# The last projection before the MLP in another order of tiles, its operand step in two parts, and new banks and loads between the MLP's two products

## The chip, the cores and the metric

One core of a Trainium2 chip runs the whole program. The metric is device time in microseconds (us), lower is better. The kernel before takes 3272.2 us (median of 3 runs, 3271.38 to 3275.03).

## The reference, cut to what matters

A decoder of two layers over 1024 tokens of width 1024. A layer has a mixing part, a cross attention and an MLP; each ends in a projection, a norm and an addition to x:

```python
        xa = cross_attention(rms_norm(x, norm_xa_pre[l]), ..., xa_wo[l])   # ends in o @ xa_wo
        x = x + rms_norm(xa, norm_xa_post[l])
        hid = jnp.square(jax.nn.relu(rms_norm(x, norm_mlp_pre[l]) @ mlp_w1[l]))
        x = x + rms_norm(hid @ mlp_w2[l], norm_mlp_post[l])
```

The change touches the way from `o @ xa_wo` into the product with `mlp_w1`, and the step from there to the product with `mlp_w2`.

## The kernel before

**Numbers.** Every matrix product is made of three matmuls, since each operand is split into a high part (a cast on ScalarE, L197) and a low part (the rest, a subtraction on VectorE, L198). A matmul of this kind is 128x128 by 128x512.

**Order.** The kernel is written as Python generators that are run one after the other or in turns (`seq(mix, xattn, after, mlp)`), over a framework that sets semaphores, gives out buffers and orders the instructions of each engine. It goes by the order of the text, but an instruction whose inputs and buffers are expected to be ready may be placed ahead of earlier ones that are not. Buffers have a tag with a fixed number of slots (`self.nb`, L101: `h` 16, `r` 16, `wr` 2, `wh` and `wl` 5, `x` 2, `xs` 2, `g` 2), and the eight banks of PSUM have the tags `d` (2), `u` (4) and `r` (2) (L102). A new buffer waits until one of its tag is free.

**The last projection** is `out_proj` (L333) with `xa_wo`, for eight tiles of 128 tokens and two halves n of 512 columns, that is 16 products of 24 matmuls. The operands of tiles 0 to 3 are formed before; those of tiles 4 to 7 (`load`, `mt`, slots of tag `r`) on the way. Half 0 makes n=0 for tiles 0 to 3, then n=1. Half 1 makes n=1 for tiles 4 to 7 first, into the banks `u`, and then n=0 for tiles 4 to 7, into the banks `d`. The n=1 weights lie in eight slots of tag `r`. When both halves of a tile are there, it is loaded (`load_x`), normed and added (`post_norm`, L295: two squares on ScalarE into a junk bank of tag `r`, a power on GpSimd, L307 and L309 on VectorE), stored, and scaled for the MLP (`scaled`, L270, into a slot `xs`: a square, GpSimd, L277). Then it is queued in `late`.

**From the queue into the MLP.** Tiles 0 to 3 are only transposed and split (`turn`, L287). The first MLP product works on 2x2 blocks by a scheme of seven products (Strassen's, in Winograd's form), and so needs, for tiles 4 to 7, sums of blocks: B22, T1, T2, T3, T4. `mlp_turn` (L1390) forms them for one tile: eight transposes into two banks of tag `r` (L1403), sums with the operands of tile tt-4 (L1415 to L1425), and a split of each of the five. It works in the tile's own `xs` slot, and reads the first of the two banks a last time at L1421. In half 1, tile 4 goes through it before the post-norm of tile 6, tile 5 before that of tile 7; 6 and 7 go through it in `finish` (L321), which makes 10 steps of the MLP (`FIN`, L30) before each.

**The MLP's first product** (`mlp`, L1429) has 16 groups g. The first two of a group's seven products, `p1` and `p2`, need only tiles 0 to 3, so for g = 0, 1, 2 these are made first, 12 matmuls each, while tiles 6 and 7 are still missing; their banks are `u`, and the weights of g = 1, 2 are loaded into slots of tag `x` (`first_weights`, L1447). Then `group` makes the five others: banks `u` for S1, S4, S2, S3 and `r` for A22, whose result VectorE takes at L1544. During group 15, `ahead` (L1643) loads and splits the first operands of the second product: `araw` from the stored hidden values `hd`, `braw` from `mlp_w2`.

**The MLP's second product** runs over blocks b and seven products each (`prods`, by the same scheme; those of b = 0 have 24 matmuls in four banks j). `sums` (L1624) forms T2, T3, T4 of the weights, on VectorE for b = 0 and on GpSimd after. The banks are chosen at L1715. The result of b = 0 is copied to `acc` by ScalarE (L1732).

All DMAs named here go through SP's queue (L137), which issues in order.

Of the kernel before, what the change touches and what calls it, by code (L numbers as in the profile page):

```python
# [8 lines left out]
F32R = mybir.dt.float32r  # L9
BF16 = mybir.dt.bfloat16  # L10
AF = mybir.ActivationFunctionType
ALU = mybir.AluOpType
# [74 lines left out]
class Kern:  # L87
# [245 lines left out]
    def out_proj(self, w, src, gpost, gpre, xin, xout, tw, tag, dst, nxt, n_nxt, first=None, early=False, pst=("uuuu", "d", "r"), turn=None):  # L333

        ws = [[], []]

        def weights(n):
            for kp in range(4):
                u = self.wunit(w[n, kp], tags=("wh", "wl") if n == 0 else (tw, tw))
                ws[n].append(tuple(t.rearrange("p (k c) -> p k c", k=2) for t in u))  # L340

        weights(0)
        yield
        gp = gn = None
        late = []

        def products(ps, n, m, ks, start, stop):
            for k in ks:
                wh, wl = ws[n][k // 2]
                self.mm3m(ps, m[0][:, k], m[1][:, k], wh[:, k % 2], wl[:, k % 2], k == start, k == stop)  # L350
                if k != ks[-1]:
                    yield

        def load(tt, i0, i1, m):
            raw = self.slot("wr", (128, 2 * (i1 - i0), 128), name="mraw")
            for i in range(i0, i1):
                self.dma(raw[:, 2 * (i - i0):2 * (i - i0) + 2],
                         src[i][:, :, 128 * tt:128 * tt + 128].rearrange("a p t -> p a t"))
            self.split(m[0][:, 2 * i0:2 * i1], m[1][:, 2 * i0:2 * i1], raw)

        operand = lambda: tuple(self.slot(tw, (128, 8, 128), F32R, name="mt") for _ in range(2))
        for half in range(2):
            ops, y0 = [], []
            if half == 0 and early:
                for j in range(4):
                    ops.append(operand())
                    load(j, 1, 4, ops[j])
                    y0.append(self.psum(pst[0][j]))
                    yield from products(y0[j], 0, ops[j], range(2, 8), 2, None)
                    if j < 3:  # L370
                        yield
                yield "wait"
                raw = self.slot("wr", (128, 2, 512), name="mraw")
                self.dma(raw, src[0][:, :, 0:512].rearrange("a p t -> p a t"))
                for j in range(4):
                    self.split(ops[j][0][:, 0:2], ops[j][1][:, 0:2], raw[:, :, 128 * j:128 * j + 128])
                    yield from products(y0[j], 0, ops[j], range(2), None, 1)
                    yield
            order = [0, 1] if half == 0 or not turn else [1, 0]
            for i in range(len(y0) // 4, 2):  # L380
                n = order[i]
                for j in range(4):
                    tt = 4 * half + j
                    if i == 0 and half == 0 and first:
                        ops.append(first[j])
                    elif i == 0:
                        ops.append(operand())
                        load(tt, 0, 4, ops[j])
                    elif ws[1] == []:
                        weights(1)  # L390
                        gp = self.gain(*gpost)
                        gn = self.gain(*gpre)
                    elif half == 1 and j == 0:
                        next(nxt)
                    ps = self.psum(pst[1] if i else pst[0][j])
                    yield from products(ps, n, ops[j], range(8), 0, 7)
                    if i == 0:
                        y0.append(ps)
                    else:
                        if half == 1 and turn and len(late) > 1:  # L400
                            self.turn_late(late, dst, tag, pst[2], turn)
                        x = self.load_x(xin, tt)
                        self.post_norm(*(y0[j], ps)[::1 if n else -1], x, gp, pst[2])
                        self.dma(xout[tt], x)
                        late.append((self.scaled(x, gn), tt))
                    if len(late) > 2 or late and i == 0:
                        self.turn_late(late, dst, tag, pst[2], turn)
                    yield
        self.finish(late, dst, tag, pst[2], nxt, n_nxt, turn)
# [977 lines left out]

    def mlp_turn(self, xs, tt, pst, X):  # L1390

        V, A, P, T = self.nc.vector, self.nc.scalar, self.nc.gpsimd, self.nc.tensor
        cs = slice(128 * (tt % 4), 128 * (tt % 4) + 128)
        if tt == 4:
            pair = lambda tag: [tuple(self.slot(tag, (128, 2, 512), F32R, name="hT") for _ in range(2)) for _ in range(2)]
            X[1] = {name: pair(tag) for name, tag in (("B22", "h"), ("T1", "h"), ("T2", "r"), ("T3", "r"), ("T4", "r"))}
        x = X[1]
        pt = []
        for b in range(2):
            pt.append(self.psum(pst, (128, 4, 128), "pt"))  # L1400
            for j in range(4):
                k = 4 * b + j
                T.transpose(pt[b][:, j, :], xs[:, k * 128:(k + 1) * 128], self.ident)  # L1403
        b12, b22 = pt
# [9 lines left out]
        for j in range(2):  # L1414
            V.tensor_tensor(two(f, j), two(b12, j), low[j][0], ALU.subtract)  # L1415
            V.tensor_tensor(two(f, j), two(f, j), low[j][1], ALU.subtract)
        split("B22", b22)
        V.tensor_tensor(t2, b22, f, ALU.subtract)
        split("T1", f)
        A.copy(f, b12)  # L1420
        V.tensor_tensor(f, b22, f, ALU.subtract)  # L1421
        split("T2", t2)
        for j in range(2):
            V.tensor_tensor(two(t2, j), low[2 + j][0], two(t2, j), ALU.subtract)
            V.tensor_tensor(two(t2, j), two(t2, j), low[2 + j][1], ALU.add)  # L1425
        split("T3", f)
        split("T4", t2)

    def mlp(self, l, hT, gpost, gpre, xin, xout, dst, nxt):  # L1429
        nc = self.nc  # L1430
# [192 lines left out]

        def sums(b, name):  # L1624

            E = P if b else V
            for u in range(len(blocks[b])):
                r = lambda n: rawB[b, n][u]
                if name == "T2":
                    b11, b12, b22 = (r(n) for n in ("B11", "B12", "B22"))  # L1630
                    E.tensor_tensor(b11, b12, b11, ALU.subtract)
                    rawB.setdefault((b, "T1"), []).append(b11)
                    t = self.slot("g", name="t2")
                    E.tensor_tensor(t, b22, b11, ALU.subtract)
                elif name == "T3":
                    t = r("B12")
                    E.tensor_tensor(t, r("B22"), t, ALU.subtract)
                else:
                    t = r("B21")
                    E.tensor_tensor(t, t, r("T2"), ALU.subtract)  # L1640
                rawB.setdefault((b, name), []).append(t)

        def ahead():  # L1643

            load_a(0, 0)
            load_b(0, "B11")
            yield
            split_a(0, 0)
            split_b(0, 0)
            load_a(1, 0)  # L1650
            load_b(0, "B21")
            yield
            load_b(0, "B22")
            yield
            load_b(0, "B12")
            yield

        for g in range(NG):
# [42 lines left out]
        for n, (b, i, p) in enumerate(prods):  # L1701
# [8 lines left out]
            if b == 3:  # L1710
                fold(*folds.get(p, ()))
                if i == 5:
                    gp = self.gain(*gpost)
                    gn = None if last else self.gain(*gpre)
            banks = [self.psum("u" if n % 2 else "ddrr"[j]) for j in range(4)]  # L1715
            for j in range(4):
                if j < 2:
                    split_a(n + 1, j)
# [65 lines left out]
    def layer(self, l, hT, vfirst, first, pj):  # L1784
# [67 lines left out]
        def ret():  # L1852
            while tm[0] < RET0 or tm[1] < RETQ:
# [10 lines left out]
        mlp = self.mlp(l, hM, (l, 5), None if l == L - 1 else (l + 1, 0), x[2], x[3], hN, nxt and nxt[0])  # L1864
        tiles = []
        after = self.out_proj(I["xa_wo"][l], od, (l, 3), (l, 4), x[1], x[2], "r", "h", hM, mlp, FIN[2], tiles,
                              turn=lambda xs, tt, pst: self.mlp_turn(xs, tt, pst, hM))
# [153 lines left out]
```

## Time and profile before

| | |
|---|---|
| median of 3 runs | 3272.2 us |
| the profiled execution's own time | 3271.57 us |
| its span | 3269.8 us |
| TensorE matmuls busy | 3116.0 us (95%), 17888 instructions |
| VectorE busy | 2098.6 us (64%) |
| ScalarE busy | 1307.2 us (40%) |
| GpSimd busy | 804.6 us (25%) |
| mean granted TensorE clock | 0.978 |

The profile is of one execution. Times in its views are us from the span's start, unless marked ns. PE is TensorE, DVE VectorE, ACT ScalarE, POOL GpSimd, SPq the sequencer that issues DMAs. In a name, out<-in are the program's buffers; a line (L198) can be that of a helper, and then the buffers tell whose work it is. The granted clock is the share of TensorE's full clock (2.4 GHz) that it was given; its low level is half of that.

### The profile page before, as it was taken

Reading aid. Unit: us, or ns where it says so; the run is one execution under the profiler, and the core shown is the slowest. Engines: PE = TensorE matmul, PEld = TensorE weight load, DVE = VectorE, ACT = ScalarE, POOL = GpSimd, SP = SyncE. Lnnn points to the kernel's source line nnn. Section 1 sums busy time; section 2 is a strip of 40 time slices with the busy share of each in tenths; the row PEclk is TensorE's granted clock in tenths of the full one; section 3 lists DMA queues with packets and bytes.
Section 4 is the critical chain, followed back from the end, with each engine's and each line's share of the span. In section 5 each row is a group of like instructions: output and inputs, shape, how many; then the busy total and the mean of one; then the engine's idle time right before and its main releaser. Section 6 shows DMA issues by size and latency. Waiting matters only on the chain. (4 is left out here: it accounts for less than half of the span.)

```text
span 3269.8 us, 47116 instructions
## 1 busy us (share of the span) xinstructions
PE 3116.0 (95%) x17888; PEld 2526.2 (77%) x17888; DVE 2098.6 (64%) x3424; ACT 1307.2 (40%) x2396; POOL 804.6 (25%) x654
## 2 busy tenths in 40 slices
PE   8999999999998999899999999999999889999998
PEld 6777777878876888788777677778788768878886
DVE  4566567364457766888835765673644666668896
ACT  5345444343433222533433454443444432235332
POOL 1000121010014786333000001210100148853330
PEclk9999999999998999999999999999999999999999
DMA  5322363252333445544433234632523334455433
GB/s 176 103 85 91 112 201 110 75 189 73 110 110 107 157 152 183 176 164 138 140 131 111 97 88 116 201 94 97 168 78 97 116 114 152 154 176 196 156 132 125
DMA packets 220995, 429.31 MB, mean 131 GB/s; under 512 B 51136, under 2 KB 98368, under 8 KB 220768
## 3 DMA queue, kind: packets, MB, share of 16 engines
q1 hardware_dynamic: 214112, 409.32, 37.7%
q0 software_dynamic: 6656, 16.98, 2.1%
q8 instruction: 141, 2.31, 0.3%
q14 instruction: 86, 0.70, 0.1%
HBM read 294.51 MB, written 131.69 MB: 130 GB/s over the span
## 5 line engine op out<-in xcount | busy, mean ns | idle before, releaser
L212 PE MATMUL p<-hT,wl 128*128 128x512 f32 x1536 | 605.0, 395 | 17.2 <-DVE wl L198 17.0
L210 PE MATMUL p<-hT,wh 128*128 128x512 f32 x1536 | 615.7, 401 | 4.7 <-ACT mc L1526 2.5
L211 PE MATMUL p<-hT,wh 128*128 128x512 f32 x1536 | 605.1, 394 | 0.0
L198 DVE TENSOR_TENSOR wl<-wraw,wh 128x1024 fp32r<-128x1024 f32 (+1 forms) x230 | 281.2, 1223 | 346.6 <-ACT wh L197 345.9
L197 ACT CAST wh<-wraw 128x1024 fp32r<-128x1024 f32 (+1 forms) x230 | 240.0, 1044 | 487.7 <-POOL wraw L1472 182.4
L246 PE MATMUL p<-bo,ao 128*128 128x512 f32 x912 | 358.0, 393 | 15.7 <-DVE mb L1544 15.7
L248 PE MATMUL p<-bo,ao 128*128 128x512 f32 x912 | 357.2, 392 | 3.9 <-DVE bo L198 3.9
L247 PE MATMUL p<-bo,ao 128*128 128x512 f32 x912 | 357.4, 392 | 0.0
L212 PEld LDWEIGHTS p<-hT,wl 128*128 128x128 f32 x1536 | 291.8, 190 | 84.1 <-DVE wl L198 22.3
L210 PEld LDWEIGHTS p<-hT,wh 128*128 128x128 f32 x1536 | 292.1, 190 | 79.1 <-issue 13.2
L211 PEld LDWEIGHTS p<-hT,wh 128*128 128x128 f32 x1536 | 292.2, 190 | 57.5 <-issue 0.7
L246 PEld LDWEIGHTS p<-bo,ao 128*128 128x128 f32 x912 | 172.7, 189 | 52.6 <-DVE mb L1544 16.6
L246 PE MATMUL p<-wh,mt 128*128 128x512 f32 x512 | 204.6, 400 | 2.6 <-ACT wh L197 1.5
L248 PEld LDWEIGHTS p<-bo,ao 128*128 128x128 f32 x912 | 172.7, 189 | 40.8 <-DVE bo L198 4.7
L256 POOL TENSOR_TENSOR rs<-ssq,neghalf 128x1 f32<-128x1 f32 x48 | 26.1, 543 | 719.9 <-DVE ssq L303 533.1
L248 PE MATMUL p<-wl,mt 128*128 128x512 f32 x512 | 201.8, 395 | 0.6 <-DVE wl L198 0.5
L247 PE MATMUL p<-wh,mt 128*128 128x512 f32 x512 | 201.6, 394 | 0.0
L247 PEld LDWEIGHTS p<-bo,ao 128*128 128x128 f32 x912 | 172.6, 189 | 35.7
L198 DVE TENSOR_TENSOR ao<-araw,ao 128x1024 fp32r<-128x1024 f32 x106 | 173.2, 1634 | 14.1 <-ACT ao L197 14.0
L198 DVE TENSOR_TENSOR bo<-braw,bo 128x1024 fp32r<-128x1024 f32 x92 | 146.8, 1600 | 44.7 <-ACT bo L197 44.7
L197 ACT CAST bo<-braw 128x1024 fp32r<-128x1024 f32 x92 | 96.6, 1052 | 186.1 <-PE p L247 124.7
L197 ACT CAST ao<-araw 128x1024 fp32r<-128x1024 f32 x106 | 111.5, 1052 | 107.5 <-DMA araw<-hd 91.3
(393 smaller groups left out, 6303.8 us busy)
## 6 DMA issues: line engine op xcount, KB each, us to landing
araw<-hd SPq DMA_DIRECT2D x106, 512.0 KB, 4.0
x<-x SPq DMA_DIRECT2D x80, 512.0 KB, 3.5
wraw<-in_mlp_w SPq DMA_DIRECT2D x68, 512.0 KB, 3.5
braw<-in_mlp_w SPq DMA_DIRECT2D x64, 512.0 KB, 4.7
wraw<-in_w_fm SPq DMA_DIRECT2D x32, 512.0 KB, 3.8
pj<-spl SPq DMA_DIRECT2D x64, 256.0 KB, 2.1
hd<-mb SPq DMA_DIRECT2D x64, 256.0 KB, 2.5
hd<-mc SPq DMA_DIRECT2D x64, 256.0 KB, 2.0
```

Of the source, the lines that this page charges most:

```text
L197: self.nc.scalar.copy(h, src)
L198: self.nc.vector.tensor_tensor(lo, src, h, ALU.subtract)
L210: mm(ps, wh, xl, start=first, stop=False)
L211: mm(ps, wh, xh, start=False, stop=False)
L212: mm(ps, wl, xh, start=False, stop=last)
L246: mm(ps, xl, wh, start=first, stop=False)
L247: mm(ps, xh, wh, start=False, stop=False)
L248: mm(ps, xh, wl, start=False, stop=last)
L256: P.tensor_tensor(r, ss, self.neghalf[:, 0:k], ALU.pow)
```

## The change

- `out_proj`: half 1 of the projection into the MLP is a function of its own. The order of products is (4, n=1), (4, n=0), (5, 1), (5, 0), (6, 1), (7, 1), (6, 0), (7, 0). The banks' tags stay: n=1 in `u`, n=0 in `d`.
- `mlp_turn` gets a `part`. Part A makes the transposes, B22 and T1; part B makes T2, T3 and T4, and gets b22-b12 as t2 minus the operands of tile tt-4 in place of a copy of the bank. A of tile 4 stands after (5, 0), A of tile 5 and B of both after (7, 1). Tiles 6 and 7 go through the whole step as before. The MLP's first step (`next(nxt)`) moves from before (4, 0) to before (6, 0).
- `ahead`: the loads for the second MLP product stand one step later, the four of `braw` together and in another order.
- `sums`: T3 and T4 of block 0 on GpSimd.
- L1715: the first two products of the second MLP matrix get the banks `ddru` and `uuur`; those after stay at `ddrr` and `uuuu` in turn.

```diff
+        def second(operand, load, products, late):
+            ops, y = {}, {}
+            for tt, n in ((4, 1), (4, 0), (5, 1), (5, 0), (6, 1), (7, 1), (6, 0), (7, 0)):
+                if n:
+                    ops[tt] = operand()
+                    load(tt, 0, 4, ops[tt])
+                if (tt, n) == (6, 0):
+                    next(nxt)
+                ps = self.psum(pst[1] if n == 0 else pst[0][tt - 4])
+                yield from products(ps, n, ops[tt], range(8), 0, 7)
+                if n:
+                    y[tt] = ps
+                    if late and late[0][1] < 4:
+                        self.turn_late(late, dst, tag, pst[2])
+                else:
+                    if tt == 5:
+                        turn(late[0][0], 4, pst[2], "A")
+                    x = self.load_x(xin, tt)
+                    self.post_norm(ps, y[tt], x, gp, pst[2])
+                    self.dma(xout[tt], x)
+                    late.append((self.scaled(x, gn), tt))
+                if (tt, n) == (7, 1):
+                    turn(late[1][0], 5, pst[2], "A")
+                    for _ in range(2):
+                        turn(*late.pop(0), pst[2], "B")
+                yield
...
-            order = [0, 1] if half == 0 or not turn else [1, 0]
-            for i in range(len(y0) // 4, 2):
-                n = order[i]
+            if half == 1 and turn:
+                yield from second(operand, load, products, late)
+                break
+            for n in range(len(y0) // 4, 2):
+                i = n
...
-    def mlp_turn(self, xs, tt, pst, X):
+    def mlp_turn(self, xs, tt, pst, X, part=None):
...
+        if tt == 4 and part == "A":
+            X[1] = {name: pair("h") for name in ("B22", "T1")}
+        if tt == 4 and part == "B":
+            X[1].update({name: pair("r") for name in ("T2", "T3", "T4")})
...
-        A.copy(f, b12)
-        V.tensor_tensor(f, b22, f, ALU.subtract)
-        split("T2", t2)
...
+        if part != "B":
...
+            split("B22", b22)
+            V.tensor_tensor(t2, b22, f, ALU.subtract)
+            split("T1", f)
+        if part is None:
+            A.copy(f, b12)
+            V.tensor_tensor(f, b22, f, ALU.subtract)
+        if part != "A":
+            split("T2", t2)
+            if part:
+                for j in range(2):
+                    for t in low[j]:
+                        V.tensor_tensor(two(f, j), two(f if t is low[j][1] else t2, j), t, ALU.subtract)
+            for j in range(2):
+                V.tensor_tensor(two(t2, j), low[2 + j][0], two(t2, j), ALU.subtract)
+                V.tensor_tensor(two(t2, j), two(t2, j), low[2 + j][1], ALU.add)
+            split("T3", f)
+            split("T4", t2)
...
-            E = P if b else V
+            E = P if b or name != "T2" else V
...
         def ahead():
 
+            yield
             load_a(0, 0)
-            load_b(0, "B11")
+            for name in ("B11", "B21", "B12", "B22"):
+                load_b(0, name)
             yield
             split_a(0, 0)
             split_b(0, 0)
             load_a(1, 0)
-            load_b(0, "B21")
-            yield
-            load_b(0, "B22")
-            yield
-            load_b(0, "B12")
             yield
...
-            banks = [self.psum("u" if n % 2 else "ddrr"[j]) for j in range(4)]
+            banks = [self.psum(("ddru", "uuur", "ddrr", "uuuu")[n if n < 2 else 2 + n % 2][j]) for j in range(4)]
```

## Rows read from the trace of the kernel before

**Rows 1.** Busy time by stretch: length, PE, PEld, DVE, ACT, POOL, PEclk, DMA, GB/s.

```profile
953.00:969.30 16.30, 16.30 (x77) 13.59 (x76) 11.27 (x21) 6.14 (x17) 2.64 (x6) 1.00 0.38 130
969.30:1011.20 41.90, 27.31 (x98) 20.70 (x97) 39.52 (x89) 26.29 (x61) 2.83 (x6) 0.76 0.20 68
...
1304.00:1324.00 20.00, 11.46 (x39) 8.88 (x38) 16.62 (x17) 7.74 (x11) 2.18 (x1) 0.74 0.53 180
...
2598.40:2639.80 41.40, 26.51 (x97) 19.90 (x96) 39.02 (x88) 26.23 (x61) 2.82 (x6) 0.75 0.20 65
...
2932.00:2951.00 19.00, 11.82 (x46) 9.30 (x45) 16.62 (x18) 7.37 (x10) 2.17 (x1) 0.82 0.55 201
```

**Rows 2.** TensorE's waits from 940 to 1012: total, times, longest.

```profile
PE p L212 <- DVE wl L198: 7.3, 2, 4.9
PE pt L1403 <- DVE xsn L1421: 6.9, 2, 5.6
```

**Rows 3.** TensorE in order of time, layer 0: start, length, [idle before, releaser].

```profile
963.00 1.03 PE L1403 MATMUL pt<-ident,xsn 128*128 128x128 f32 x8
...
969.33 0.39 PE L210 MATMUL p<-hT,wh 128*128 128x512 f32 x1
...
982.92 1.94 PE L1403 MATMUL pt<-ident,xsn 128*128 128x128 f32 x8 [5.56 <-DVE xsn L1421]
985.18 0.79 PE L210 MATMUL p<-hT,wh 128*128 128x512 f32 x1 [0.32 <-ACT wh L197]
...
989.70 0.80 PE L212 MATMUL p<-hT,wl 128*128 128x512 f32 x1 [2.44 <-DVE wl L198]
...
1011.17 0.39 PE L210 MATMUL p<-hT,wh 128*128 128x512 f32 x1
```

**Rows 4.** VectorE in order of time, same stretch.

```profile
953.04 0.70 DVE L307 TENSOR_TENSOR p<-p,gain 128x512 f32<-128x512 f32 x1 [15.37 <-ACT junk L300]
...
958.20 1.28 DVE L277 SCALAR_TENSOR_TENSOR xsn<-x,rs,gain 128x1024 f32<-128x1024 f32 x1 [2.22 <-POOL rs L256]
...
975.63 0.42 DVE L198 TENSOR_TENSOR hT<-xsn,hT 128x256 fp32r<-128x256 f32 x1
...
978.28 1.28 DVE L277 SCALAR_TENSOR_TENSOR xsn<-x,rs,gain 128x1024 f32<-128x1024 f32 x1 [0.55 <-POOL rs L256]
...
980.41 1.42 DVE L198 TENSOR_TENSOR hT<-xsn,hT 128x256 fp32r<-128x256 f32 x4
...
988.43 1.21 DVE L198 TENSOR_TENSOR wl<-wraw,wh 128x1024 fp32r<-128x1024 f32 x1
```

**Rows 5.** TensorE in order of time at the border of the MLP's products.

```profile
1304.33 0.39 PE L246 MATMUL p<-bo,ao 128*128 128x512 f32 x1
...
1308.18 0.39 PE L248 MATMUL p<-bo,ao 128*128 128x512 f32 x1
1317.11 0.79 PE L246 MATMUL p<-bo,ao 128*128 128x512 f32 x1 [8.54 <-DVE mb L1544]
...
1323.22 0.39 PE L248 MATMUL p<-bo,ao 128*128 128x512 f32 x1
```

**Rows 6.** SP's queue in order of time: when DMAs were issued.

```profile
920.00 0.33 SPq L137 DMA_DIRECT2D wraw<-in_mlp_w  x1
...
979.59 0.33 SPq L137 DMA_DIRECT2D wraw<-in_mlp_w  x1
...
1299.50 1.37 SPq L137 DMA_DIRECT2D braw<-in_mlp_w  x3
```

**Rows 7.** VectorE in order of time at the border.

```profile
1308.35 1.23 DVE L198 TENSOR_TENSOR bo<-braw,bo 128x1024 fp32r<-128x1024 f32 x1 [1.81 <-ACT bo L197]
```

**Rows 8.** The page's DMA issues: count, size, median us to landing.

```profile
wraw<-in_mlp_w SPq DMA_DIRECT2D x68, 512.0 KB, 3.5
```

**Rows 9.** VectorE and GpSimd side by side, in order of time.

```profile
1342.39 3.36 DVE L198 TENSOR_TENSOR ao<-araw,ao 128x1024 fp32r<-128x1024 f32 x1 [0.21 <-ACT ao L197]
...
1342.26 2.41 POOL L1631 TENSOR_TENSOR braw<-braw,braw 128x1024 f32<-128x1024 f32 x1 [29.82 <-DVE bo L198]
```

More of the change, by code (lines that the diff above doesn't have):

```diff
@@ L399, in out_proj @@
                     else:
-                        if half == 1 and turn and len(late) > 1:
-                            self.turn_late(late, dst, tag, pst[2], turn)
                         x = self.load_x(xin, tt)
-                        self.post_norm(*(y0[j], ps)[::1 if n else -1], x, gp, pst[2])
+                        self.post_norm(y0[j], ps, x, gp, pst[2])
                         self.dma(xout[tt], x)
@@ L1382, in xattn @@
                 next(fill, None)
-    def mlp_turn(self, xs, tt, pst, X):
+    def mlp_turn(self, xs, tt, pst, X, part=None):
         V, A, P, T = self.nc.vector, self.nc.scalar, self.nc.gpsimd, self.nc.tensor
         cs = slice(128 * (tt % 4), 128 * (tt % 4) + 128)
-        if tt == 4:
-            pair = lambda tag: [tuple(self.slot(tag, (128, 2, 512), F32R, name="hT") for _ in range(2)) for _ in range(2)]
-            X[1] = {name: pair(tag) for name, tag in (("B22", "h"), ("T1", "h"), ("T2", "r"), ("T3", "r"), ("T4", "r"))}
-        x = X[1]
[L1398 to L1404, printed above, removed]
+        pair = lambda tag: [tuple(self.slot(tag, (128, 2, 512), F32R, name="hT") for _ in range(2)) for _ in range(2)]
+        if tt == 4 and part == "A":
+            X[1] = {name: pair("h") for name in ("B22", "T1")}
+        if tt == 4 and part == "B":
+            X[1].update({name: pair("r") for name in ("T2", "T3", "T4")})
+        x = X[1]
         f, t2 = (xs[:, 512 * i:512 * i + 512].rearrange("p (k c) -> p k c", k=4) for i in range(2))
@@ L1412, in split @@
                 self.split(h, lo, two(src, j))
[L1414 to L1419, printed above, removed]
-        A.copy(f, b12)
-        V.tensor_tensor(f, b22, f, ALU.subtract)
-        split("T2", t2)
[L1423 to L1427, printed above, removed]
+        if part != "B":
+            pt = []
+            for b in range(2):
+                pt.append(self.psum(pst, (128, 4, 128), "pt"))
+                for j in range(4):
+                    k = 4 * b + j
+                    T.transpose(pt[b][:, j, :], xs[:, k * 128:(k + 1) * 128], self.ident)
+            b12, b22 = pt
+            for j in range(2):
+                V.tensor_tensor(two(f, j), two(b12, j), low[j][0], ALU.subtract)
+                V.tensor_tensor(two(f, j), two(f, j), low[j][1], ALU.subtract)
+            split("B22", b22)
[10 more added lines that the diff above has]
+                        V.tensor_tensor(two(f, j), two(f if t is low[j][1] else t2, j), t, ALU.subtract)
+            for j in range(2):
+                V.tensor_tensor(two(t2, j), low[2 + j][0], two(t2, j), ALU.subtract)
+                V.tensor_tensor(two(t2, j), two(t2, j), low[2 + j][1], ALU.add)
+            split("T3", f)
+            split("T4", t2)
     def mlp(self, l, hT, gpost, gpre, xin, xout, dst, nxt):
@@ L1866, in layer @@
         after = self.out_proj(I["xa_wo"][l], od, (l, 3), (l, 4), x[1], x[2], "r", "h", hM, mlp, FIN[2], tiles,
-                              turn=lambda xs, tt, pst: self.mlp_turn(xs, tt, pst, hM))
+                              turn=lambda xs, tt, pst, part=None: self.mlp_turn(xs, tt, pst, hM, part))
         xattn = self.xattn(l, hX, kv, od, after, tiles)
```

## The prediction, made before the changed kernel was run

> **What bounds the kernel now.** TensorE does nearly all the time, so only the stretches in which it stands still can be won. I read the table by stretch first [rows 1]. In the last projection of a layer it is busy without a gap until 969.3 us. Then, in the 41.9 us in which the projection hands over to the MLP, it is busy for 27.3, the granted clock is 0.76 on average, and VectorE is busy for 39.5: this stretch is VectorE's. It ends at 1011.17 with the 73rd MLP matmul [rows 3], the first of the five products that need the operands of tiles 4 to 7. The work ahead of it is three pairs of products of 24 matmuls and the transposes of three tiles. A matmul at full clock starts 0.2265 us after the last (18 from 1304.33 to 1308.18, [rows 5]), so 72 take 16.3; a tile's eight transposes take about 0.8 (1.03 with their overlap, [rows 3]). That makes 18.7, and the rest, **23.2 us**, is lost. Layer 1 has the same stretch (41.4, lost 22.7).
>
> The waits of TensorE say where [rows 2]: the transposes of tiles 5 and 6 wait 6.9 us for L1421, and two first matmuls of MLP groups wait 7.3 us for the low half of their weights. In TensorE's order of time [rows 3] the transposes of tile 6 start at 982.92, the products of group 1 go on at 989.70, and group 0's at 1011.17. VectorE's rows [rows 4] give the cause: it waits 15.4 us up to 953.04, and from then on four tiles' post-norms and operand formations stand in one queue. The second of a tile's two steps keeps its `xs` slot (two of them) and a bank of tag `r` (two) until late: the last split of tile 4 is at 975.63, so tile 6 is scaled only at 978.28; its x slot comes free then, so the weights of group 1 are asked for at 979.59 [rows 6], and their split stands behind tile 5's until 988.43 [rows 4].
>
> The second place is the border of the two MLP products. TensorE stands still for 8.5 us up to 1317.11 [rows 5], though the product begun at 1304.33 has its operands. Its fourth bank is the second `r`, and that one waits for L1544, the end of the last group; the 14 matmuls from there to 1323.22 take 6.1 instead of 14 x 0.2265 = 3.2, so 2.9 more go to the clock (granted 0.74, [rows 1]). In layer 1, 19.0 - 11.8 = 7.2 us stand idle, and some 1.6 go to the clock. VectorE reached L1544 late because splits waiting for `braw` stood ahead of it: the whole end of the group stands behind a split that starts at 1308.35 after 1.8 us of waiting [rows 7]; three of those loads were issued together at 1299.50 [rows 6].
>
> All that can be won is 23.2 + 22.7 + 11.4 + 8.8 = 66 us.
>
> **The order of the eight products.** One takes 24 x 0.2265 = 5.44. Until now the n=0 products were fifth to eighth; now tile 4's is second, tile 5's fourth, tiles 6 and 7 stay last. No matmul is added. With the start at 920, tile 4 is complete at about 935 instead of 952, tile 5 at 946.5 instead of 957.5, tile 6 at 964.5 and tile 7 at 970. VectorE's idle stretch before 953.04 takes the two post-norms (2.7 each: two multiplies at 0.6, two adds at 0.66, the sum) and two scalings at no cost. From a first multiply to the scaled tile go 953.04 to 959.48, 6.4 us [rows 4], so tile 4 is scaled by 942.5 and tile 5 by 957, the transposes being due at 946.6 and 958.3. The margin of tile 5 is thin: part A of tile 4 holds both `r` banks for about 1.5 us, and the post-norm's squares need one. A slip there costs 0 to 2 us; I take 0.
>
> **Operands in two parts.** VectorE starts a 256-wide operation every 0.33 us (four in 1.42, [rows 4]) and a 512-wide one every 0.6. Part A is 8 x 0.33 + 0.6 = 3.3, part B 14 x 0.33 = 4.7; the whole step was 18 x 0.33 + 2 x 0.6 = 7.2. So 2 x 0.8 = 1.6 us of VectorE are added, and a copy of ScalarE goes. Part A of tile 5 and both parts B come at 958.3, after the last n=1 product, since T3 and T4 need the slots of the n=1 weights. There 3.3 + 2 x 4.7 = 12.7 us are due; some 3 of tile 4's part B need no such slot and fit before. So VectorE has 9.4 to 12.7 us in front of the post-norm of tile 6, which is ready at 965.5: the queue ends at 968.5 to 972. With 2.7 for the post-norm and 3.5 for the scaling (from its last add), tile 6 is scaled at 974.5 to 978; I take 975, against 979.56 now, with its banks free.
>
> **What then is late.** The two products of group 0 end at 975.5, and the transposes of tile 6 follow at once. The weights of group 1 come next: x slot free at 975, load 3.5 [rows 8] to 4.5 (asked for at 979.59, [rows 6]; cast before 985.18, [rows 3]), cast 1.05, split 1.2, so TensorE goes on at 980 to 981.5 instead of 989.7. This stall of 4 to 5 us stays, and with it some 2 us of slower clock. Then VectorE has until the start of group 0's five products: post-norm 7 and two scalings 5.1, three additions 1.8, tile 6's step 7.2, two weight splits 2.4, the sums of group 0's weights 3.0, part of tile 7's step 3.3 and one more split 1.1, together 24 from 972: **996** instead of 1011.2. The third wait, for group 2's weights, goes. Gain 15; bounds: 10, if VectorE runs with gaps as long as today's, and 18, if TensorE alone set it with that one stall. I take 14 for each layer, **28**. What follows in groups 1 and 2 is tied to the same splits and moves along.
>
> **The border.** The first product of the second MLP matrix gets one bank of `u` in place of the second `r`, the next three of `u` and one `r`. With VectorE as late as today, that second product would begin at 1309.8 and meet L1540 and L1544 in its third and fourth bank at about 1315 and 1317: a stall of 3 instead of 8.5. This is the least gain, 5.5 and part of the clock. But the four `braw` loads now stand together, right behind the first product of group 15, whose operands' slots they take, and no longer in three steps; that product ends at about 1288 (six products of 2.7 us ahead of 1304.33), and at about 3 us each they land by 1303, and VectorE's wait [rows 7] shrinks. I leave 2 us lost per layer: gain 9.4 and 6.8, **16**; bounds 5.5 to 11.4 and 4 to 8.8.
>
> **Two sums on GpSimd.** T3 and T4 of the first block leave VectorE (2 x 1.13) for the idle GpSimd; they are needed two or three products, over 10 us, later. A row speaks against it: a 1024-wide split of VectorE takes 3.36 us beside GpSimd's L1631 of 2.41 [rows 9], and 1.21 alone [rows 4]. So each moved sum may cost VectorE 2.1 where it saves 1.1: 2 us per layer if that were on the path; against that, one product takes 5.4 us and needs 2.3 of VectorE, which hides it. I take 0.
> The Trainium skill (SBUF — State Buffer, "Who interferes with whom") has a rule for this row: a VectorE instruction with two SBUF inputs and a GpSimd one that reads SBUF exclude each other for a whole instruction. The trace agrees (3.36 is about 2.41 + 1.21 less some overlap). By the rule as by the row the sum would be 4 us higher for both layers if nothing hid it.
>
> **Rivals.**
> (a) *VectorE's queue moves, it doesn't shrink.* Parts A and B run ahead of tile 6's post-norm with gaps, tile 6 is scaled at 978 or later and the stalls of today stay but for 4 us a layer: 8 + 16 = 24, so 3248. For it: VectorE gets 1.6 us more work and 12.7 stand at one place. Against it: 15.4 idle microseconds earlier are used.
> (b) *The border stays VectorE's.* The u banks of the second product wait for the same late chain, 5.5 + 4: 28 + 9.5, so 3234.
> (c) *Slower: the operand loads stand behind the store of x.* In the text of the new function the loads for tile 5 come after the store of tile 4's x. If SP's queue kept that order, the product would wait for the post-norm (1.2 of squares and 2.7), the load, the cast and the split (3.5 + 1.05 + 1.2): 9.7 us before tile 5 and again before tile 6, with 2.9 of clock each as at the border, 25 us a layer, 50 in all against gains of 28 to 44, so 3278 to 3294, about 3285. It decides as soon as one of these loads is queued behind such a store. Against it: today the first weights of the MLP, written down after the fourth product (946), are issued at 920.00 [rows 6], so queues are filled by readiness, not by the order of the text.
>
> **How the numbers follow.** The profiled execution took 3271.57 (median 3272.2, 0.6 more, which I leave). 3271.6 - 28 - 16 = **3227**. Chances: forecast 0.60, (a) 0.14, (b) 0.14, (c) 0.07, nothing measurable 0.05. The forecast's own range is 20 + 9.5 to 36 + 20, 3216 to 3242; with (a) and (b) the range is 3214 to 3252. About 0.2% can be told from no change (6.5 us); faster 0.87, same 0.06, slower 0.07.
>
> **What would show it.** Right: TensorE's wait for L1421 at tile 6 gone; the time from the last projection matmul to group 0's five products 26 us instead of 41.9, with one stall of 4 to 5 us for `wl` in it; the wait for L1544 under 3 us. Wrong: waits of the projection's matmuls for `mt` (c), the transposes of tile 5 or 6 waiting for a scaled tile (a), the second product at the border waiting for L1534, L1540 or L1544 for over 3 us (b), or VectorE's share in the handover still over nine tenths of 40 us.

## The result, and the profile after

The changed kernel takes **3238.95 us** (median of 4 runs, 3237.09 to 3242.41) against 3271.79 for the kernel before beside it (4 runs, 3270.51 to 3275.03): ratio 0.9901, 95% interval 0.9889 to 0.9912, or 32.8 us less. The forecast was 3227. Run again among the experiments (after_again) it took 3240.9 against 3274.59, 33.7 less. The profiled execution took 3239.32, with a span of 3237.5.

I read the new profile by two stretches. **Handover**: from the start of the first MLP matmul after the projection to the start of the 73rd (967.37 to 996.38 in layer 0; 969.33 to 1011.17 before [rows 3]). **Border**: the first 168 matmuls of the second MLP product, from the start of the first to that of the 169th; at full clock and without a wait they take 168 x 0.2265 = 38.1. All such times are differences of starts in TensorE's rows.

| us, layer 0 / layer 1 | before | after | after_again |
|---|---|---|---|
| last eight products of the projection | 49.1 / 49.1 | 49.9 / 50.3 | 49.9 / 50.2 |
| handover | 41.8 / 41.4 | 29.0 / 30.5 | 31.0 / 29.1 |
| from there to the second MLP product | 293.2 / 293.5 | 293.9 / 293.2 | 293.2 / 293.9 |
| border | 49.8 / 47.1 | 45.0 / 42.9 | 43.9 / 44.3 |

The first two lines lost 21.8 us together (21.2 in after_again), where the prediction has 28; the border lost 9.0 (8.6 there), where it has 16. That is 30.8 of the 32.3 by which the spans differ; both terms have the right sign and come out at 0.78 and 0.56 of their size.

Busy time by stretch of the changed kernel; columns as in [rows 1], which it answers. The first line is the handover, the second the part of it from where the prediction lets VectorE's last queue begin, the others are the borders.

```profile
967.37:996.38 29.01, 22.32 (x89) 17.06 (x88) 25.50 (x51) 18.68 (x40) 2.10 (x5) 0.88 0.27 93
970.00:996.38 26.38, 19.69 (x78) 14.86 (x77) 24.32 (x49) 16.35 (x34) 1.57 (x4) 0.87 0.25 82
1290.00:1310.00 20.00, 15.67 (x59) 12.38 (x59) 20.00 (x18) 11.59 (x16) 7.87 (x3) 0.83 0.62 205
2905.00:2924.00 19.00, 16.14 (x64) 12.85 (x63) 19.00 (x17) 10.53 (x14) 7.91 (x3) 0.91 0.66 234
```

VectorE does 25.5 us of work in the handover instead of 39.5, and its share of that stretch is still nearly nine tenths. At the border it is busy for the whole 20 us, and GpSimd for 7.9 instead of 2.2: that is new.

TensorE's waits of the changed kernel from 940 to 1000 (answering [rows 2]): total, times, longest.

```profile
PE p L212 <- DVE wl L198: 4.0, 1, 4.0
PE p L210 <- ACT wh L197: 2.6, 1, 2.6
```

The wait of tile 6's transposes for the second step's last read (L1421, now L1454) is gone, and no transposes of the operand step wait any more: 14.2 us of waits became 6.6. The two that are left are for the first weights of group 1 (high part) and of group 2 (low part).

TensorE in order of time, in the handover (answering [rows 3]) and from 1298 on at the border (answering [rows 5]):

```profile
967.14 0.39 PE L248 MATMUL p<-wl,mt 128*128 128x512 f32 x1
967.37 0.39 PE L210 MATMUL p<-hT,wh 128*128 128x512 f32 x1
...
972.82 1.03 PE L1444 MATMUL pt<-ident,xsn 128*128 128x128 f32 x8
976.43 0.61 PE L210 MATMUL p<-hT,wh 128*128 128x512 f32 x1 [2.58 <-ACT wh L197]
...
990.13 0.64 PE L212 MATMUL p<-hT,wl 128*128 128x512 f32 x1 [4.03 <-DVE wl L198]
990.57 0.63 PE L210 MATMUL p<-hT,wh 128*128 128x512 f32 x1
991.00 0.63 PE L211 MATMUL p<-hT,wh 128*128 128x512 f32 x1
...
1298.20 0.39 PE L248 MATMUL p<-bo,ao 128*128 128x512 f32 x1
1302.92 0.80 PE L246 MATMUL p<-bo,ao 128*128 128x512 f32 x1 [4.33 <-DVE ma L1578]
...
1306.07 0.63 PE L247 MATMUL p<-bo,ao 128*128 128x512 f32 x1
1306.50 0.63 PE L248 MATMUL p<-bo,ao 128*128 128x512 f32 x1
```

The 36 matmuls from 1290.27 to 1298.20 run without a gap, through the place where TensorE stood for 8.5 us before. Then, 12 matmuls into the next product, it stops for 4.33 (2.9 in layer 1) for L1578, the old L1540. After each stop the matmuls start 0.43 apart instead of 0.2265: ten times from 1303.51 on, eight times from 990.13 on. The clock granted there is the low level: 0.50 from 1303.5 to 1307.3 and 0.52 from 990.2 to 993.5. So a stop of 4 us costs some 2 more.

VectorE in order of time, in the handover (answering [rows 4]) and from 1291 on at the border (answering [rows 7]). It begins tile 6's scaling at 970.28; the split that TensorE waits for at 990.13 begins at 988.86. The one at 993.86 is of the weights for the first of group 0's five products.

```profile
970.28 1.28 DVE L277 SCALAR_TENSOR_TENSOR xsn<-x,rs,gain 128x1024 f32<-128x1024 f32 x1 [1.29 <-POOL rs L256]
...
985.50 1.64 DVE L198 TENSOR_TENSOR hT<-xsn,hT 128x256 fp32r<-128x256 f32 x4
987.06 0.68 DVE L1510 TENSOR_TENSOR wraw<-wraw,wraw 128x512 f32<-128x512 f32 x1
987.66 0.68 DVE L1548 TENSOR_TENSOR mb<-p,ma 128x512 f32<-128x512 f32 x1
988.26 0.68 DVE L1511 TENSOR_TENSOR wraw<-wraw,wraw 128x512 f32<-128x512 f32 x1
988.86 1.22 DVE L198 TENSOR_TENSOR wl<-wraw,wh 128x1024 fp32r<-128x1024 f32 x1
...
993.86 1.21 DVE L198 TENSOR_TENSOR wl<-wraw,wh 128x1024 fp32r<-128x1024 f32 x1
...
1291.28 3.10 DVE L1672 TENSOR_TENSOR t<-braw,braw 128x1024 f32<-128x1024 f32 x1
1294.31 1.21 DVE L198 TENSOR_TENSOR bo<-braw,bo 128x1024 fp32r<-128x1024 f32 x1
1295.44 0.68 DVE L1572 TENSOR_TENSOR ma<-p,ma 128x512 f32<-128x512 f32 x1
1296.04 2.82 DVE L198 TENSOR_TENSOR ao<-araw,ao 128x1024 fp32r<-128x1024 f32 x1
1298.79 1.75 DVE L1574 TENSOR_TENSOR mc<-mc,ma 128x512 f32<-128x512 f32 x1
...
1302.19 0.68 DVE L1578 TENSOR_TENSOR ma<-p,ma 128x512 f32<-128x512 f32 x1
```

GpSimd in order of time, at the border:

```profile
1290.90 2.40 POOL L1675 TENSOR_TENSOR braw<-braw,braw 128x1024 f32<-128x1024 f32 x1 [14.95 <-DVE braw L1669]
1294.52 3.26 POOL L1678 TENSOR_TENSOR braw<-braw,t 128x1024 f32<-128x1024 f32 x1 [1.21 <-ACT ao L197]
1297.74 2.24 POOL L1573 TENSOR_TENSOR mc<-mc,ma 128x512 f32<-128x512 f32 x1
```

The last lines of VectorE and these belong together. While the two moved sums run on GpSimd (L1675 is T3, L1678 is T4), two operations of VectorE take 3.10 and 2.82, where such a one takes 1.21 alone [rows 4]: 3.5 us in the queue that ends in L1578. The Trainium skill (SBUF — State Buffer, "Who interferes with whom") says that a VectorE instruction with two inputs in SBUF contends with a GpSimd instruction that reads SBUF, and that one with at most one such input does not. The trace agrees with both: L1672 and the split have two, and L1572, one of whose inputs is a bank of PSUM, took 0.68 beside L1678, as ever.

SP's queue in order of time (answering [rows 6]):

```profile
971.59 0.33 SPq L137 DMA_DIRECT2D wraw<-in_mlp_w  x1
973.72 0.32 SPq L137 DMA_DIRECT2D x<-x  x1
...
977.35 0.38 SPq L137 DMA_DIRECT2D wraw<-in_mlp_w  x1
...
1280.29 2.04 SPq L137 DMA_DIRECT2D braw<-in_mlp_w  x4
```

The weights of group 1 are asked for 0.03 us after tile 6 is scaled (970.28 + 1.28). The four `braw` loads stand together, 10 us ahead of the border.

### The profile page after: what moved, and what is told of

Its sections match the earlier page's. It is cut to its first block, busy times and chain, and to the rows that moved or that the text cites. A ratio compares the mean times of both kernels' runs of the same rounds, so it can differ in the third digit from the quotient of the medians.

```text
span 3237.5 us, 47152 instructions
## 1 busy us (share of the span) xinstructions
PE 3111.1 (96%) x17888; PEld 2522.3 (78%) x17888; DVE 2102.0 (65%) x3432; ACT 1302.7 (40%) x2392; POOL 815.7 (25%) x658
## 3 DMA queue, kind: packets, MB, share of 16 engines
q1 hardware_dynamic: 214112, 409.32, 38.1%
## 5 line engine op out<-in xcount | busy, mean ns | idle before, releaser
L198 DVE TENSOR_TENSOR bo<-braw,bo 128x1024 fp32r<-128x1024 f32 x92 | 146.4, 1595 | 29.3 <-ACT bo L197 29.2
```

## The experiments

Each kernel is compared with the kernel before on the same chip; these medians are 3272.48 for e1 to e4, 3272.87 for e5 to e9 without e7, and 3274.59 for the others, and the column of gains is against them.

| kernel | us | gain | ratio, 95% interval | handover | border |
|---|---|---|---|---|---|
| e1_turn_only | 3250.58 | 21.9 | 0.9938, 0.9923 to 0.9953 | 28.2 / 29.7 | 49.2 / 49.4 |
| e2_border_only | 3262.95 | 9.5 | 0.9969, 0.9959 to 0.9978 | 41.6 / 41.8 | 45.2 / 42.9 |
| e3_sums_vector | 3243.91 | 28.6 | 0.9913, 0.9898 to 0.9927 | 31.9 / 28.3 | 46.1 / 42.2 |
| e4_old_banks | 3253.62 | 18.9 | 0.9944, 0.9929 to 0.9959 | 30.5 / 29.3 | 50.3 / 49.3 |
| e5_weight_sums_gpsimd | 3241.08 | 31.8 | 0.9901, 0.9885 to 0.9918 | 31.2 / 30.9 | 45.0 / 42.6 |
| e6_order_without_parts | 3246.29 | 26.6 | 0.9921, 0.9907 to 0.9936 | 31.4 / 33.2 | 40.5 / 41.2 |
| e8_sums_vector_banks | 3233.90 | 39.0 | 0.9884, 0.9869 to 0.9899 | 28.9 / 30.5 | 40.3 / 38.1 |
| e9_no_load_group1 | 3235.45 | 37.4 | 0.9890, 0.9871 to 0.9905 | 27.6 / 28.4 | 44.7 / 42.9 |
| e10_banks_alone | 3241.13 | 33.5 | 0.9894, 0.9880 to 0.9909 | 30.6 / 30.5 | 43.8 / 41.9 |
| e7_old_loads | 3251.34 | 23.3 | 0.9929, 0.9912 to 0.9945 | 31.0 / 29.8 | 49.8 / 46.8 |
| e8_again | 3236.34 | 38.3 | 0.9883, 0.9866 to 0.9899 | 30.5 / 28.8 | 39.4 / 38.2 |
| after_again (the changed kernel) | 3240.90 | 33.7 | 0.9896, 0.9881 to 0.9911 | 31.0 / 29.1 | 43.9 / 44.3 |

In nine profiles (the changed kernel's two and all but e2, e5, e6 and e9) the program of the handover is the same; its 18 times lie between 28.2 and 31.9, mean 29.9. The border of the changed kernel differs by up to 1.5 between its two profiles. Differences within this scatter carry nothing here.

### The two halves by themselves

e1 keeps the new projection and the parts, with the border as before; e2 is the reverse (the functions of the projection and `mlp_turn` as before, `ahead`, `sums` and the banks as changed).

```diff
# e1: against the changed kernel; ahead() as before, too
-            E = P if b or name != "T2" else V
+            E = P if b else V
-            banks = [self.psum(("ddru", "uuur", "ddrr", "uuuu")[n if n < 2 else 2 + n % 2][j]) for j in range(4)]
+            banks = [self.psum("u" if n % 2 else "ddrr"[j]) for j in range(4)]
```

> The kernel before with the new order of the projection's products and the operand step in two parts; the border between the MLP's products as it was. In the traces the two handovers of the changed kernel are 11.4 and 10.2 us shorter than before. If the two halves of the change are independent: 3271.8 - 21.6 = 3250, within 3. Rival, that the handover's gain needs the new loads or banks of the border as well (they share slots and SP's queue): 3258 or more.

> The kernel before with the border alone: new banks, the four braw loads together, two sums on GpSimd. In the traces the two borders are 4.8 and 4.5 us shorter. Independent halves: 3271.8 - 9.3 = 3262.5, within 3. If the prediction's size for the border (16) holds without the other half: 3256.

Measured: 21.9 and 9.5 us of gain, 31.4 together against 32.8 for both at once. Within the scatter the halves are independent, and the two terms of the prediction can be judged apart.

### The border: sums, banks and loads

**e3**: T3 and T4 of block 0 back on VectorE, nothing else.

```diff
-            E = P if b or name != "T2" else V
+            E = P if b else V
```

> The changed kernel with the two sums T3 and T4 of block 0 back on VectorE. Theory: the prediction costed them at 0 on GpSimd, but they run while VectorE works off the end of the last group (a sum there took 3.10 instead of 1.21, a split 2.82 instead of 1.22), and TensorE waits 4.3 and 2.9 us for that work. Then the wait falls to about 1 and 0 us, with up to 2 of clock each: 3239 - 6 to 10 = 3229 to 3233. Rival: VectorE's 2 x 1.13 more are worse than the collision: 3239 to 3244, with the wait for the end of the group as long or longer.

Measured: no gain over the changed kernel (28.6 against 32.8). The wait for L1578 falls from 4.33 to 0.47, as the collision theory says, but the border stays at 46.1 / 42.2, because TensorE stops at the next place. TensorE of e3, in order of time:

```profile
1303.47 0.50 PE L246 MATMUL p<-bo,ao 128*128 128x512 f32 x1 [0.47 <-DVE ma L1578]
...
1314.67 0.79 PE L246 MATMUL p<-bo,ao 128*128 128x512 f32 x1 [3.72 <-ACT acc L1767]
```

The third product's banks are `ddrr`; its last bank is the one from which ScalarE (L1767) still has to copy the second product's last result. That copy stands in ScalarE's queue behind a cast whose load has not landed. ScalarE of e3:

```profile
1310.68 1.04 ACT L197 CAST ao<-araw 128x1024 fp32r<-128x1024 f32 x1 [3.53 <-DMA araw<-hd]
1311.63 0.58 ACT L1767 COPY acc<-p 128x512 f32<-128x512 f32 x1
1312.10 1.05 ACT L197 CAST bo<-braw 128x1024 fp32r<-128x1024 f32 x1
1313.05 1.56 ACT L1767 COPY acc<-p 128x512 f32<-128x512 f32 x3
```

So my expectation failed in one step: that the stop, once gone, has no successor.

**e8** adds to e3 the remedy for that successor: the third product and those after it get `ddru` and `uuur` in turn, so that no product's last bank is the one that the product ahead of it used last. **e10** makes that edit alone, with the sums left on GpSimd.

```diff
-            banks = [self.psum(("ddru", "uuur", "ddrr", "uuuu")[n if n < 2 else 2 + n % 2][j]) for j in range(4)]
+            banks = [self.psum(("ddru", "uuur")[n % 2][j]) for j in range(4)]
```

> The kernel with the two sums on VectorE (the run before, 3243.9), and the banks d, d, r, u and u, u, u, r in turn for all products, so that the third product doesn't need the bank that ScalarE empties last. Theory: in that run the wait for the end of the group was gone (0.5 us), and the third product's fourth bank waited 3.7 us for a copy on ScalarE that stood behind a cast waiting for its load; with the new banks this wait goes, and the next is the fourth product's operand, some 1.5 us: 5 us less than that run in both layers, 3239 or below. Rival, that the late operands set the pace whatever bank is used: 3243 to 3245, with the same microseconds at the fourth product.

> The changed kernel with its two sums T3 and T4 left on GpSimd, and the banks of the fastest experiment (letters ddru and uuur in turn for all products after the second, too). It separates that experiment's two edits. My theory (GpSimd's sums hold up VectorE's row of instructions): the matmul that waits for the copy of the second part in L1578 still waits 4.3 us in the first layer and 2.9 in the second, the first 168 matmuls of the second product take 45.0 and 42.9 us as in the changed kernel, and the time stays at 3239 us (3237 to 3241). Rival (the banks alone bring the gain, the sums nothing): these waits go, the 168 matmuls take about 40 and 38 us, and the time is 3234 us.

Measured: e8 has a border of 40.3 / 38.1 and gains 39.0 us. ScalarE still stands for the same load (3.60 in e8, 3.53 in e3), but the third product no longer needs a bank that a copy behind it has to free. e10 gains 33.5, as the changed kernel does, and TensorE's wait at the border stays; in layer 0 of e10 (3.2 in layer 1):

```profile
PE p L246 <- DVE ma L1578: 4.0, 1, 4.0
```

Each edit alone brings nothing that can be measured, both together take 9 to 10 us off the border: two stops in a row, the second of which shows only once the first is gone. That the collision makes the first is shown by e3 and e8, where it goes with the two sums. VectorE in the second profile of e8, the same stretch:

```profile
1295.15 1.21 DVE L1672 TENSOR_TENSOR t<-braw,braw 128x1024 f32<-128x1024 f32 x1
1296.28 1.22 DVE L198 TENSOR_TENSOR bo<-braw,bo 128x1024 fp32r<-128x1024 f32 x1
...
1301.08 1.21 DVE L1675 TENSOR_TENSOR braw<-braw,braw 128x1024 f32<-128x1024 f32 x1
...
1302.81 0.67 DVE L1578 TENSOR_TENSOR ma<-p,ma 128x512 f32<-128x512 f32 x1
```

From the start of L1672 to that of L1578 go 7.7 us here, with T3 (L1675) among them on VectorE itself, and 10.9 in the changed kernel.

**e8 and the changed kernel side by side:**

> The fastest experiment once more (sums T3 and T4 on VectorE, banks ddru and uuur in turn), beside the changed kernel itself on the same chip. Theory: it is 4 to 7 us faster than the changed kernel (3234 against 3239), the second product's first 168 matmuls at about 40 and 38 us against 45 and 43. Rival (its lead is the scatter of the handover from run to run, 28 to 32 us for the same program): the two are within 2 us of each other.

> The changed kernel unedited, beside the experiment above on the same chip, to compare the two without the kernel before in between, and to see how far its own stages scatter. Theory: 3238 to 3240 us, handover 28 to 32 us in each layer, the second product's first 168 matmuls 45.0 and 42.9 us within 0.5. Rival (the stage of the second product scatters as the handover does): these differ from the first profile by over 1 us.

Measured: 3236.34 (3231.49 to 3237.36) against 3240.90 (3237.21 to 3244.88), 4.6 us less; over the two pairs the gains are 39.0 and 38.3 against 32.8 and 33.7. e8 is the fastest of all kernels here. Its border is shorter by 9.5 and 10.6 in the two pairs of profiles, its time by 5 to 6; where the other 4 go was not settled. The spans of the two pairs differ by 3.7 and 13.4, since stages that no edit touches differ too: at 384 us, long ahead of all edits, e8's first profile is 4.8 us behind the changed kernel's. Of the last expectation the rival came true: the border moved by 1.1 and 1.5 between the changed kernel's two profiles, though its sum over both layers only by 0.4.

**e4**: all as changed but the banks. **e7**: all as changed but `ahead`. (The expectation of e7 puts these loads ahead of the first MLP product. That is wrong: `ahead` loads for the second.)

```diff
# e4
+            banks = [self.psum("u" if n % 2 else "ddrr"[j]) for j in range(4)]
# e7
-            yield
             load_a(0, 0)
-            for name in ("B11", "B21", "B12", "B22"):
-                load_b(0, name)
+            load_b(0, "B11")
             yield
             split_a(0, 0)
             split_b(0, 0)
             load_a(1, 0)
+            load_b(0, "B21")
+            yield
+            load_b(0, "B22")
+            yield
+            load_b(0, "B12")
```

> The changed kernel with the old banks (d, d, r, r and then u) for the first two products of the second MLP matrix. Theory: then the first product's fourth bank waits for the last operation of group 15, in the changed trace at 1304.6, from about 1294 on: a wait of 10 instead of 4.3, so 5 us more in each layer: 3249. Rival: the loads alone bring the gain, and the banks change nothing: 3239, with a wait in the trace of 4 to 5 us.

> The changed kernel with the loads ahead of the first MLP product in their old order (tile by tile over four turns, instead of all behind the second turn). Theory (the loads' place matters because the weight load of a group stands behind them on SyncE's queue): the handover grows by 1 to 2 us in each layer, to 31 to 32 us, and the time is 3241 to 3243 us. Rival (the queue of VectorE sets the handover, and the loads land in time in either order, so their order is worth nothing): the handover stays at 28 to 32 us, and the time at 3237 to 3241.

Measured: without the new banks the whole border gain is gone (50.3 / 49.3; TensorE waits 9.69 for L1582, the old L1544), and without the new loads nearly all of it (49.8 / 46.8), 10.4 us of time. Both expectations of e7 fell: they look at the handover, which didn't move. TensorE, SP's queue and ScalarE of e7:

```profile
1305.15 0.79 PE L246 MATMUL p<-bo,ao 128*128 128x512 f32 x1 [4.16 <-DVE ma L1578]
...
1317.56 0.50 PE L246 MATMUL p<-bo,ao 128*128 128x512 f32 x1 [3.70 <-ACT acc L1770]
...
1307.50 0.80 SPq L137 DMA_DIRECT2D hd<-mc  x2
1309.27 0.32 SPq L137 DMA_DIRECT2D araw<-hd  x1
...
1313.57 1.04 ACT L197 CAST ao<-araw 128x1024 fp32r<-128x1024 f32 x1 [6.65 <-DMA araw<-hd]
```

The loads' place doesn't shorten the wait for L1578 (4.16 against 4.33). What it removes is the second stop, the one of e3: in e7 an `araw` load is issued at 1309.27, behind the store of `mc` at 1307.50, which waits for VectorE's end of the last group, and ScalarE's queue stands for 6.65 us at the cast of such a load. In the changed kernel two `araw` loads are issued from 1298.89 on, ahead of that store (1304.02). ScalarE stands 6.11 us for the first of them too, but until 1302.52, while TensorE waits for L1578 anyway. The loads' place alone does not decide it: in e3, which has the new place, one `araw` load still comes behind that store (1306.31, the store at 1304.58), and that is the load for which ScalarE stands there.

### The handover: what sets its 29 us

**e9** leaves out the load of group 1's first weights and uses those of group 0 in their place, so the values of group 1 are others. If the wait for an x slot set the handover, it would fall far.

```diff
-            raw = self.slot("x", name="wraw")
-            self.dma(raw, W[l, 2 * g])
+            if g == 1:
+                raw = raw0[0]
+            else:
+                raw = self.slot("x", name="wraw")
+                self.dma(raw, W[l, 2 * g])
```

> The changed kernel with the first weights of group 1 not loaded: they are split from group 0's in their place, so the values of group 1 are not the reference's and the work stays the same but for one load of 512 KB in each layer. The load has to wait until tile 6 is scaled, since it takes that tile's x slot; now it doesn't, and group 2's takes the slot. Theory that the x slots set the handover: both waits for weights go with their clock, 5 and 6 us in each layer: 3217. Rival, that VectorE's queue sets it (in the changed trace the split of group 0's S weights ends at 995.1 and the products that need it start at 995.9): the waits move, at most 1 to 3 us per layer are won: 3233 to 3237.

**e5** relieves VectorE: the four sums of group 0's weights go to GpSimd.

```diff
-            E = P if g else V
+            E = P
```

> The changed kernel with the four sums of group 0's weights (0.6 us each) on GpSimd, as those of the other groups are. In the changed trace three of them and the additions stand in VectorE's queue ahead of the split of group 2's weights (started at 988.86, TensorE goes on at 990.13 after a wait of 4.0). Theory that VectorE's queue sets the handover: it gets 2.4 us shorter, the wait for that split falls to about 2, and the 73rd MLP matmul comes 2 us earlier in each layer: 3235. Rival, that GpSimd's reads hold up VectorE's operations by as much as they save, as at the border: 3239 to 3243.

Measured: the slot theory fell. e9's handover is 27.6 / 28.4, 1.9 below the mean of 29.9, and its gain 4 us larger. The wait for group 1's weights is gone, but one of 2.3 comes in its place, and that for group 2's stays. TensorE of e9:

```profile
985.56 2.17 PE L1444 MATMUL pt<-ident,xsn 128*128 128x128 f32 x8 [2.34 <-ACT xsn L1453]
991.28 0.80 PE L212 MATMUL p<-hT,wl 128*128 128x512 f32 x1 [3.56 <-DVE wl L198]
```

VectorE is busy for 29.7 of 31 us there. GpSimd doesn't help it, though: in e5 the handover is 31.2 / 30.9, the wait for group 2's weights 5.7, and splits beside the moved sums take longer. VectorE of e5:

```profile
987.09 2.79 DVE L198 TENSOR_TENSOR hT<-xsn,hT 128x256 fp32r<-128x256 f32 x2
```

GpSimd of e5:

```profile
986.88 1.29 POOL L1510 TENSOR_TENSOR wraw<-wraw,wraw 128x512 f32<-128x512 f32 x1
988.25 1.35 POOL L1511 TENSOR_TENSOR wraw<-wraw,wraw 128x512 f32<-128x512 f32 x1
```

Two such splits take 0.75 in the changed kernel. The collision is the one of the border. No run took work from VectorE here without putting reads by GpSimd beside it, so that VectorE's queue sets these 29 us is read from the rows, not shown by an experiment.

**e6** keeps the new order of products and makes the operands of tiles 4 and 5 in one step each, both after the product (7, 1).

```diff
-                    if tt == 5:
-                        turn(late[0][0], 4, pst[2], "A")
...
-                    turn(late[1][0], 5, pst[2], "A")
                     for _ in range(2):
-                        turn(*late.pop(0), pst[2], "B")
+                        turn(*late.pop(0), pst[2])
```

> The changed kernel with the new order of products but the operand step in one piece: tiles 4 and 5 whole, one behind the other, after the product (7, n=1), where only now the slots of T3 and T4 are free. Theory that the two parts carry the gain with the order: 14.4 us of VectorE then stand ahead of tile 6's post-norm instead of some 9, the transposes of tile 5 wait for tile 4's banks, and tile 6 is scaled 4 to 5 us later: 5 us more per layer, 3249. Rival, that the order alone brings it: 3239 to 3242.

Measured: between the two expectations, nearer to the theory's: 6 us less gain than the changed kernel. The handover is 31.4 / 33.2, the groups after it take 296.7 / 295.2 (293 to 294 in the others), and TensorE waits 3.8 for tile 6's scaling. The border of e6 is shorter by 3 on average: VectorE's queue with the two moved sums is as long there (10.95 us), but TensorE comes to it nearly 3 us later, measured against that queue, and stops for 1.6 (2.4 in layer 1). So a part of what is lost ahead of the border comes back at it, and 6 us of time is what the parts are worth net of that.

## Why the prediction's two terms came out smaller

The time lies within the range given for the forecast, 3216 to 3242, but near its upper end, 12 us above the forecast; rival (b)'s 3234 is nearer. The two terms don't make up for each other: both have the right sign and both are too large. Within the handover some luck is left, as a stall that was put down came out shorter and one that was left out came.

**What bounded the kernel**: right, as far as the rows tell. VectorE's queue set the handover. The change took 14 us of its work out of that stretch (39.5 to 25.5), and 12 and 10 us of time went with it, net of the 0.8 and 1.2 by which the projection's last eight products grew, in which tile 5's transposes now stand.

**Order and parts**: right. The projection ends 2.0 us earlier on the trace's clock than before (967.37 against 969.33); with that added, tile 6 is scaled at 973.5, where the prediction has 975. VectorE's last queue was put at 24 us; it was 24.3 (the second line of the first fence).

**Handover 28, measured 22**: the step that failed is "the third wait, for group 2's weights, goes". It stayed, at 4.0, and cost some 2 more of slow clock. Group 2's weights are cast by 984.4, but their split begins at 988.86: tile 6's last splits, two weight sums and L1548 stand ahead of it in VectorE's queue. The stall that the sum did keep, 4 to 5 us for group 1, was 2.6. And VectorE's 24 us were laid end to end, from 972 to 996; VectorE stood still for 2.1 of them (26.38 - 24.32, mostly for the short steps of ScalarE and GpSimd in the scalings). The five products began at 996.38 + 1.96 = 998.3, 2.3 later than the 996 of the prediction. The two delays overlap: the split that the first of them needs (that of 993.86) ends at 995.07, and TensorE, which runs without a wait from 990.13 on, comes 1.3 later. So the third wait accounts for some 1.3 of the 2.3 (in layer 1 that split ends at 2611.83, and TensorE comes at 2613.80), and VectorE's own pauses for the rest. Layer 0's gain of 12.0 lies within the bounds of 10 to 18, layer 1's of 9.8 just below.

**Border 16, measured 9**: that banks and loads decide there was right, and each is needed (e4, e7). The term that failed is the two sums on GpSimd, for which the prediction says "I take 0". The row for it was quoted, with its price of 2.1 for each sum, and set aside since one product takes 5.4 us and needs 2.3 of VectorE. That compares averages; the two sums fell into the 11 us of VectorE's queue between L1672 and L1578, where it has no slack. They cost 3.5 there, and with it the stops of 4.3 and 2.9 and the slow clock behind them. Nor did the sum look for the stop after that one (e3). With both put right in e8, the border is 18.5 us shorter than before (19.2 in e8_again), more than the 16 of the forecast. The 4.8 of layer 0 lie below their bounds of 5.5 to 11.4. Rival (b) tells what came, a stop at L1540 of over 3 us and 9.5 us in all, but with late loads as its cause, where it is GpSimd.

**Loads**: the reason given was that VectorE's wait for `braw` shrinks. It does: in e7 two splits between the first product's start and L1578 come after pauses of 2.14 and 1.16, in the changed kernel there is none. But L1578 starts 11.8 us after the first matmul of the border in e7 and 11.9 in the changed kernel, so that brought nothing beside the collision. What the place brought is told by e7: in the changed kernel it puts an `araw` load ahead of a store that waits for VectorE, and ScalarE's queue doesn't stand for it when the third product needs its bank.

**Rival (c)**: absent. Between 900 and 1000 TensorE waits for no `mt`. **Rival (a)**: the transposes of tiles 5 to 7 do not wait. Its premise, that VectorE stays the bound, holds all the same as far as the rows tell, over a shorter stretch.

## What to carry to other kernels

An engine that is idle isn't free: before work moves from VectorE to GpSimd, look at what VectorE does in just that stretch, and where those are operations with both inputs in SBUF, add GpSimd's length to the path. A stall that is removed is worth only what lies before the next one in the same chain: name that next one (here the bank that the following product needs, and the engine that frees it) and try both edits together, since each alone may show nothing. Where a queue issues in order, a load's place against the stores that wait for compute can count for more than the time it takes to land.

## What the runs showed of the hardware that I had not expected

- Where the two engines exclude each other, whichever comes second loses: L1678 on GpSimd took 3.26 when VectorE's split had begun 0.2 us before it, against 2.40 for L1675, and L1573 2.24 behind a split and 1.29 in e8.
- A cast that waits for a load holds everything behind it in ScalarE's queue, the copies that free PSUM banks too: 3.53 us in e3, 6.65 in e7. TensorE stood 3.72 and 3.70 for such a copy.
- The handover of one and the same program took 28.2 to 31.9 us, while the eight products ahead of it took 49.9 to 50.3. A stage that three engines and a load set in turn scatters by a tenth.
